# A hybrid decoder layer: attention as the second side stream, its gate first, gate transfers on GpSimd's queue, other pauses

## The chip, the cores and the metric

One core of a Trainium2 chip runs the whole kernel. The metric is the device time of one execution in microseconds, as the median of several runs. The engines are TensorE (PE), VectorE (DVE), ScalarE (ACT), GpSimd (POOL) and SyncE (SP, which here only issues DMAs).

## The reference

One decoder layer for 2048 prompt tokens and 8 x 4 sample tokens that share weights, all in float32:

```
proj = x @ w_in
q, k, v, g_a, u_b, g_b, x_c, g_c, g_m = split(proj)
attn = banded attention with sinks and relative bias, window 128     (branch a)
z    = gelu(S5 state space of u_b);  y_b = z * sigmoid(z @ w_glu)      (branch b)
y_c  = RG-LRU(causal conv4 of x_c)                                     (branch c)
ya = (attn * silu(g_a)) @ w_br_a;  yb = (y_b * silu(g_b)) @ w_br_b;  yc = (y_c * silu(g_c)) @ w_br_c
merged = sigmoid(g_m)[a] * ya + sigmoid(g_m)[b] * yb + sigmoid(g_m)[c] * yc
y = layernorm(alpha * x + merged @ w_out)
```

Outputs are y and the new caches and states.

## The kernel before

Float32 products are made of three passes: each operand is split into a high and a low part (`split`, L91 to L96: ACT makes the high part, DVE the low one), and `mm3` (L98 to L101) adds high by high, low by high and high by low.

Phase 1 is the input projection. `TILES` lists 50 tiles of 128 output columns; for each, `gemm` runs five units of tokens (512, 512, 512, 272, 272), each of 8 x 3 matmuls, with the tile's split weights against the split x, which stays in SBUF. `w_load` and `w_split` bring the next tile's weights (one "wh" on ACT and one "wl" on DVE a tile). `evac` empties PSUM: "m" tiles (the merge gates) take one ACT tanh and go to DRAM from ACT's queue; the gate tiles "gc", "gb", "ga" take an ACT tanh and two DVE products (one with PSUM, one with the branch's output, which `gate_load` has fetched into "br" a unit ahead), and go to DRAM with the next unit (`gate_st`). Both transfers are issued on SP (`LD`).

Beside it run four side streams, written as generators: `s5_stream`, `glu_stream`, `lru_stream`, `attn_stream`. Their matmuls are put between the main ones: after every three main matmuls `tick` adds their ideal time to a counter, and when it passes the pause that the last `yield` asked for (`STEP` 4.6 us where none is given), `side_step` runs the first stream in `sides` to its next `yield`. So the list `sides` and the pauses set the order of all queues; every engine then works in that order and waits by semaphores.

```
            sides += [glu_stream(), lru_stream(), attn_stream()]
```

An attention step `n` (block `n // 2`, key head `n % 2`) issues the scores of `n` ("sa", L1025 and L1026), the value products of `n - 2` ("sb", L1100, which read the copies "pth", "ptl", "ptq" that POOL masks), the transposes of `n - 1` ("sc", L1052, which read the softmax tile "S"), then DVE's maximum and sums, and yields `ATT_SCORE`; then ACT's exponentials and DVE's last product (`soft_norm`, L1012), and yields `ATT_SOFTMAX`. In odd steps `prep` also makes the high and low parts of the next block's queries and keys (the low parts "q" and "kl" on DVE). GLU runs 8 columns `j` in two halves; the first half of `j + 1` needs the split z ("zh", "zl") that `gelu_b` makes right behind the second half of `j`. RG-LRU makes 5 chunks of matmuls for each of 4 blocks, and then a chain of long ACT and DVE instructions with a scan of 2104 elements.

While the last gate runs, `seam` loads and splits the first branch's operands for phase 2 (`y_unit`: branch projections and merge) and phase 3 (`out_mm`, `out_ln`: output projection and layer norm).

Of the kernel before, what the change touches and what calls it, by code (L numbers as in the profile page):

```python
# [30 lines left out]
GLU_WEIGHTS = 2.0  # L31
ATT_SCORE, ATT_SOFTMAX = 2.5, 3.5
# [5 lines left out]
         + [("gc", i) for i in range(4)] + [("gb", i) for i in range(4)] + [("ga", i) for i in range(4)])  # L38
# [15 lines left out]
def kernel(ctx: ExitStack, tc: tile.TileContext, I, O):  # L54
# [62 lines left out]
    stage = ph1.enter_context(tc.tile_pool(name="stage", bufs=3))  # L117
# [20 lines left out]
    sides, a_done, prompt_done, pace, hold = [], [False], [False], [0.0, STEP], [0]  # L138
# [53 lines left out]
    def evac(kind, i, u, ps):  # L192
# [19 lines left out]
        elif kind == "q":  # L212
            spill(ps, n, qD[i][:, t0:t0 + n])
        elif kind == "m":
            spill(ps, n, mD[i][:, t0:t0 + n], AF.Tanh, 0.5)
        else:
            b = kind[1]
            gt = gp[0].tile([128, 512], FT, name=uid("gt"), tag="gt", bufs=2)[:, :n]
            br = gate_br.pop((b, i, u))
            act(gt, ps[:, :n], AF.Tanh, scale=0.5)  # L220
            stt(gt, gt, 1.0, ps[:, :n], OP.add, OP.mult)
            st = stage.tile([128, 512], FT, name=uid("st"), tag="st")[:, :n]
            if b == "b":
                nch = min(n, TP - t0) // 8
                V.tensor_mul(st[:, :nch * 8].rearrange("p (c j) -> p c j", j=8),
                             gt[:, :nch * 8].rearrange("p (c j) -> p c j", j=8),
                             br[:, :, 0:nch].rearrange("p j c -> p c j"))
                if u == 4:
                    V.tensor_mul(st[:, 240:272].rearrange("p (b t) -> p b t", t=4),
                                 gt[:, 240:272].rearrange("p (b t) -> p b t", t=4),  # L230
                                 br[:, 0:4, 30:38].rearrange("p t b -> p b t"))
            else:
                V.tensor_mul(st, gt, br)
            gate_st.append((actD[b][i][:, t0:t0 + n], st))
# [442 lines left out]
    def glu_stream():  # L677
# [58 lines left out]
        for j in range(8):  # L736
# [3 lines left out]
            yield  # L740
# [6 lines left out]
            yield  # L747
# [9 lines left out]
    def lru_stream():  # L757
# [123 lines left out]
        for i in range(4):  # L881
# [29 lines left out]
            stt(b_, b_, 0.5, R, OP.mult, OP.mult)  # L911
            V.memset(aa[:, 2048:2104].rearrange("p (b s) -> p b s", s=7)[:, :, 2], 0.0)
# [14 lines left out]
    def attn_stream():  # L927
        gp.append(side_pool(ges, "gate"))
# [219 lines left out]
        prompt_done[0] = True  # L1148
# [98 lines left out]
    def x_load(u):  # L1247
        t0, n = UN[u]
        for k in range(8):
# [3 lines left out]
            xr = early.tile([128, 512], FT, name=uid("xr"), tag="xr", bufs=6)  # L1253
# [7 lines left out]
    for kk in (slice(0, 4), slice(4, 8)):  # L1261
        r = early.tile([128, 512], FT, name=uid("xr"), tag="xr", bufs=6).rearrange("p (k c) -> p k c", k=4)
        LD.dma_start(r, I["w_in"][1][:, kk])
        split(WS[1][0][:, kk], WS[1][1][:, kk], r)
# [18 lines left out]
    BR = "cba"  # L1283
# [86 lines left out]

    def gate_load(b, i, u):
        t0, n = UN[u]
        br = gp[0].tile([128, 512], FT, name=uid("br"), tag="br", bufs=3)
        if b == "b":
            c0, nch = t0 // 8, 38 if u == 4 else n // 8
            br = br[:, :8 * nch].rearrange("p (j c) -> p j c", j=8)
            LD.dma_start(br, zD[i][:, :, c0:c0 + nch])
        else:
            br = br[:, :n]
            LD.dma_start(br, (hD if b == "c" else aD)[i][:, t0:t0 + n])  # L1380
# [3 lines left out]
    for i in range(2, len(TILES)):  # L1384
        kind, ti = TILES[i]
        if kind == "x" and ti == 0:
# [4 lines left out]
            sides += [glu_stream(), lru_stream(), attn_stream()]  # L1391
        if kind == "gc":
            while not gp:
                side_step()
        if kind == "ga":
            while not prompt_done[0]:
                side_step()
# [3 lines left out]
        for p, u in enumerate(order):  # L1401
            while gate_st:
                LD.dma_start(*gate_st.pop(0))
            if (kind, ti, p) == ("ga", 0, 3):
                while sides:
                    side_step()
# [9 lines left out]
            if kind == "ga":  # L1416
# [3 lines left out]
    while gate_st:  # L1420
        LD.dma_start(*gate_st.pop(0))
# [276 lines left out]
```

## Time and profile before

| | us |
|---|---|
| median of 3 runs | 1793.37 |
| lowest and highest | 1792.03, 1796.07 |
| the profiled execution | 1796.0 |
| its span, first to last instruction | 1793.9 |
| PE, DVE, ACT, POOL busy | 1771.1, 1132.4, 654.6, 169.5 |

The profiled execution is one run with the profiler on; the span is the part of it from its first to its last instruction, 2.1 us less. In the profile a busy PE includes the time in which a matmul waits behind its weight load, so its share says where the kernel is bound, and not that every matmul is at its peak. In this run side streams occupy these stretches: S5 to about 450 us, GLU 477 to 605, RG-LRU 622 to 838, attention 851 to 1160 and its sample part to 1240; the gates begin at about 1010 us.

### The profile page before, as it was taken

How to read it: one execution, taken by the hardware profiler on the slowest of the kernel's cores; microseconds unless marked ns; L12 is line 12 of the kernel's file. 1: busy time of each engine (PE TensorE's matmuls, PEld its weight loads, DVE VectorE, ACT ScalarE, POOL GpSimd, SP SyncE). 2: the span in 40 equal slices, each digit the busy share in tenths (PEclk: the TensorE clock that was granted, in tenths of full speed). 3: DMA queues.
4: the chain of work that ended last, by engine and by line, in shares of the span. 5: the costliest groups of instructions: out<-in, count | busy, mean ns of one | idle time of the engine just before them, and what ended most of it. 6: DMA issues, size and time to landing. Idle time of an engine off the chain costs nothing. (4 is left out here: it accounts for less than half of the span.)

```text
span 1793.9 us, 26547 instructions
## 1 busy us (share of the span) xinstructions
PE 1771.1 (99%) x9748; PEld 1543.1 (86%) x9748; DVE 1132.4 (63%) x2451; ACT 654.6 (36%) x1383; POOL 169.5 (9%) x379
## 2 busy tenths in 40 slices
PE   8999999999999999999999999999999999999997
PEld 7888888888899888888988888888888888887886
DVE  5755888886333456653777899653343557667666
ACT  6312443343333287674665655311220202111110
POOL 0000000000000000000355555400000000000000
PEclk9999999999999999999999999999999999999999
DMA  7443343433333334433332334453455646542222
GB/s 235 112 135 100 111 109 111 117 107 94 120 120 115 100 94 122 105 95 102 106 102 84 119 122 132 107 165 101 143 172 153 191 127 189 183 145 97 94 95 81
DMA packets 214278, 220.36 MB, mean 123 GB/s; under 512 B 89140, under 2 KB 157108, under 8 KB 212980
## 3 DMA queue, kind: packets, MB, share of 16 engines
q1 hardware_dynamic: 182772, 169.70, 33.4%
q10 hardware_dynamic: 31376, 48.97, 7.7%
q8 instruction: 77, 1.26, 0.3%
q14 instruction: 53, 0.43, 0.1%
HBM read 136.53 MB, written 83.14 MB: 122 GB/s over the span
## 5 line engine op out<-in xcount | busy, mean ns | idle before, releaser
L99 PE MATMUL mm<-xh,wh 128*128 128x512 f32 (+1 forms) x1920 | 678.8, 354 | 0.0
L101 PE MATMUL mm<-xh,wl 128*128 128x512 f32 (+1 forms) x1920 | 673.3, 351 | 0.0
L100 PE MATMUL mm<-xl,wh 128*128 128x512 f32 (+1 forms) x1920 | 671.1, 350 | 0.0
L101 PEld LDWEIGHTS mm<-xh,wl 128*128 128x128 f32 x1920 | 361.1, 188 | 47.1 <-DVE wl L94 0.3
L99 PEld LDWEIGHTS mm<-xh,wh 128*128 128x128 f32 x1920 | 361.6, 188 | 43.6
L100 PEld LDWEIGHTS mm<-xl,wh 128*128 128x128 f32 x1920 | 361.9, 188 | 42.7
L99 PE MATMUL py<-ah,wbh 128*128 128x512 f32 (+1 forms) x480 | 169.1, 352 | 1.5 <-DVE br L104 0.8
L101 PE MATMUL py<-ah,wbl 128*128 128x512 f32 (+1 forms) x480 | 168.9, 352 | 0.0
L100 PE MATMUL py<-ah,wbh 128*128 128x512 f32 (+1 forms) x480 | 168.8, 352 | 0.0
L89 ACT ACTIVATE st<-mm 128x512 f32<-128x512 f32 (+1 forms) x170 | 86.9, 511 | 155.9 <-PE mm L101 142.6
L99 PEld LDWEIGHTS py<-ah,wbh 128*128 128x128 f32 x480 | 90.3, 188 | 15.1 <-issue 1.1
L100 PEld LDWEIGHTS py<-ah,wbh 128*128 128x128 f32 x480 | 90.3, 188 | 12.7
L101 PEld LDWEIGHTS py<-ah,wbl 128*128 128x128 f32 x480 | 90.2, 188 | 12.5
L94 DVE TENSOR_TENSOR wl<-wr,wh 128x1024 fp32r<-128x1024 f32 x48 | 58.9, 1226 | 38.0 <-ACT wh L89 37.9
L1505 PE MATMUL po<-woh,mg 128*128 128x512 f32 x256 | 79.6, 389 | 0.0
L104 DVE SCALAR_TENSOR_TENSOR br<-br,py 128x512 f32<-128x512 f32 (+1 forms) x80 | 46.8, 585 | 51.5 <-PE py L101 45.7
L104 DVE SCALAR_TENSOR_TENSOR gt<-gt,mm 128x512 f32<-128x512 f32 (+1 forms) x60 | 35.0, 584 | 69.7 <-ACT gt L89 69.5
L89 ACT ACTIVATE gt<-mm 128x512 f32<-128x512 f32 (+1 forms) x60 | 30.9, 515 | 117.4 <-PE mm L101 117.4
L1505 PE MATMUL po<-woh,mo 128*128 128x512 f32 x224 | 69.5, 389 | 0.0
L89 ACT ACTIVATE wbh<-wbr 128x512 fp32r<-128x512 f32 x24 | 15.1, 629 | 147.7 <-PE py L100 125.7
L1543 POOL TENSOR_TENSOR lr<-lr,lngb 128x192 f32<-128x192 f32 x1 | 0.6, 589 | 628.8 <-ACT lr L1542 628.8
L89 ACT ACTIVATE wh<-wr 128x1024 fp32r<-128x1024 f32 x48 | 50.5, 1052 | 23.7 <-DMA wr<-in_w_in_dram 10.0
(352 smaller groups left out, 2797.2 us busy)
## 6 DMA issues: line engine op xcount, KB each, us to landing
wr<-in_w_in_dram SPq DMA_DIRECT2D x48, 512.0 KB
mD<-st ACTq DMA_DIRECT2D x72, 256.0 KB
br<-mD SPq DMA_DIRECT2D x71, 256.0 KB
lx<-in_xr_dram SPq DMA_DIRECT2D x16, 512.0 KB
mD<-st ACTq DMA_DIRECT2D x48, 136.0 KB
br<-mD SPq DMA_DIRECT2D x47, 136.0 KB
xr<-in_xT_dram SPq DMA_DIRECT2D x24, 256.0 KB
wbr<-in_w_br_dram SPq DMA_DIRECT2D x24, 256.0 KB
```

The lines of the kernel that those rows point to most:

```text
L89: return A.activation(out, in_, func, bias=bias, scale=scale, **kw)
L94: V.tensor_sub(lo, src, hi)
L99: PE.matmul(ps, wh, xh, start=start, stop=False)
L100: PE.matmul(ps, wh, xl, start=False, stop=False)
L101: PE.matmul(ps, wl, xh, start=False, stop=stop)
L104: return (eng or V).scalar_tensor_tensor(out, a, s, b, op0=op0, op1=op1)
L1505: PE.matmul(o, m, w, start=k == 0 and q == 0, stop=k == 7 and q + 1 == len(prods))
L1543: G.tensor_mul(r[:, c], r[:, c], gb[:, 0, c])
```

## The change

`sides` becomes attention, RG-LRU, GLU, and the gate tiles come as "ga", "gc", "gb", each after its stream. The first two gates have no pool of their own: their "br" and "gt" tiles come from the stage pool (now 4 tiles), the product is written in place, and both their transfers are issued on GpSimd's queue (`G`). Pauses change: GLU 4.6 to 3.9, attention 2.5 and 3.5 to 2.2 and 3.0. RG-LRU's end gets one more `yield`. The x start-up buffers go from 6 to 5. Phase 2 takes the branches as a, c, b.

```
-GLU_WEIGHTS = 2.0
-ATT_SCORE, ATT_SOFTMAX = 2.5, 3.5
+GLU_WEIGHTS, GLU_STEP = 2.0, 3.9
+ATT_SCORE, ATT_SOFTMAX = 2.2, 3.0
...
-         + [("gc", i) for i in range(4)] + [("gb", i) for i in range(4)] + [("ga", i) for i in range(4)])
+         + [("ga", i) for i in range(4)] + [("gc", i) for i in range(4)] + [("gb", i) for i in range(4)])
...
-    stage = ph1.enter_context(tc.tile_pool(name="stage", bufs=3))
+    stage = ph1.enter_context(tc.tile_pool(name="stage", bufs=4))
...
-            gt = gp[0].tile([128, 512], FT, name=uid("gt"), tag="gt", bufs=2)[:, :n]
+            early_ = not gp
+            gt = gate_tile("gt")[:, :n]
...
-            st = stage.tile([128, 512], FT, name=uid("st"), tag="st")[:, :n]
+            st = gt if early_ else stage.tile([128, 512], FT, name=uid("st"), tag="st")[:, :n]
...
-            gate_st.append((actD[b][i][:, t0:t0 + n], st))
+            gate_st.append((G if early_ else LD, actD[b][i][:, t0:t0 + n], st))
...
             glu_mm(j, 0)
...
-            yield
+            yield GLU_STEP
             glu_mm(j, 1)
...
-            yield
+            yield GLU_STEP
...
             stt(b_, b_, 0.5, R, OP.mult, OP.mult)
+            yield 2.5
...
-            xr = early.tile([128, 512], FT, name=uid("xr"), tag="xr", bufs=6)
+            xr = early.tile([128, 512], FT, name=uid("xr"), tag="xr", bufs=5)
...
-    BR = "cba"
+    BR = "acb"
...
+    def gate_tile(tag):
+
+        if not gp:
+            return stage.tile([128, 512], FT, name=uid("st"), tag="st")
+        return gp[0].tile([128, 512], FT, name=uid(tag), tag=tag, bufs=3 if tag == "br" else 2)
+
     def gate_load(b, i, u):
         t0, n = UN[u]
-        br = gp[0].tile([128, 512], FT, name=uid("br"), tag="br", bufs=3)
+        br = gate_tile("br")
+        q = LD if gp else G
...
-            LD.dma_start(br, (hD if b == "c" else aD)[i][:, t0:t0 + n])
+            q.dma_start(br, (hD if b == "c" else aD)[i][:, t0:t0 + n])
...
-            sides += [glu_stream(), lru_stream(), attn_stream()]
-        if kind == "gc":
-            while not gp:
+            sides += [attn_stream(), lru_stream(), glu_stream()]
+        if kind[0] == "g" and ti == 0:
+
+            while len(sides) > {"a": 2, "c": 1, "b": 0}[kind[1]]:
                 side_step()
-        if kind == "ga":
-            while not prompt_done[0]:
-                side_step()
+            if kind == "gb":
+                gp.append(side_pool(ges, "gate"))
```

How the built order moves, at three places. First DVE's queue in an odd attention step (the last half of step 21): "ptl" is the low part of the transposed softmax, "q" and "kl" the low parts of the next block, "m" the sums, "S" the softmax tile, "gt" and "st" a gate's two products, "wl" a weight split. Before:

```order
L1106 TENSOR_TENSOR oo_10977<-sb_11108,oo_10977 64x2x4x64
L1059 TENSOR_TENSOR ptl_11122<-sc_11116,pth_11121 128x512
L104 SCALAR_TENSOR_TENSOR q_11098<-qr_10914,q_11098 64x256 x2
L978 TENSOR_TENSOR kl_8514<-kr_10916,k_11100 64x256
L104 SCALAR_TENSOR_TENSOR q_11099<-qr_10914,q_11099 64x256 x2
L978 TENSOR_TENSOR kl_8515<-kr_10916,k_11101 64x256
L1010 TENSOR_TENSOR m_11097<-m_11097 128x4
L1011 RECIPROCAL m_11097<-m_11097 128x4
L1012 TENSOR_TENSOR S_11096<-S_11096,m_11097 128x4x128
L104 SCALAR_TENSOR_TENSOR gt_11192<-gt_11192,mm_11151 128x512
L233 TENSOR_TENSOR st_11195<-gt_11192,br_11032 128x512
```

With the change:

```order
L1107 TENSOR_TENSOR oo_7559<-sb_7670,oo_7559 64x2x4x64
L1060 TENSOR_TENSOR ptl_7684<-sc_7678,pth_7683 128x512
L104 SCALAR_TENSOR_TENSOR q_7660<-qr_7511,q_7660 64x256 x2
L979 TENSOR_TENSOR kl_5231<-kr_7513,k_7662 64x256
L104 SCALAR_TENSOR_TENSOR q_7661<-qr_7511,q_7661 64x256 x2
L979 TENSOR_TENSOR kl_5232<-kr_7513,k_7663 64x256
L94 TENSOR_TENSOR wl_7714<-wr_7380,wh_7713 128x1024
L1011 TENSOR_TENSOR m_7659<-m_7659 128x4
L1012 RECIPROCAL m_7659<-m_7659 128x4
L1013 TENSOR_TENSOR S_7658<-S_7658,m_7659 128x4x128
L1041 TENSOR_TENSOR S_7773<-sa_7764,B 128x768
```

The gate's two products between this step's softmax and the next step's first sum are gone, and in this step a weight split stands ahead of the sums; such a row stands there in two of the sixteen odd steps.

Second, DVE's queue around the place in GLU where the split z ("zl") of the next column is made; "zy" and "zt" are GLU's own tiles, "st" here a gate's. Before:

```order
L696 TENSOR_TENSOR zt_5756<-zt_5756,zy_5692 128x1056
L104 SCALAR_TENSOR_TENSOR zy_5561<-zs_5833,zy_5561 128x528
L104 SCALAR_TENSOR_TENSOR zy_5692<-zt_5756,zy_5692 128x1056
L96 SCALAR_TENSOR_TENSOR zl_5838<-zy_5692,zh_5837 128x1056
L94 TENSOR_TENSOR wl_5863<-wr_5643,wh_5862 128x1024
L104 SCALAR_TENSOR_TENSOR zy_5692<-zs_5901,zy_5692 128x528
L107 TENSOR_SCALAR zt_5904<-zt_5904 128x1056
L696 TENSOR_TENSOR zt_5904<-zt_5904,zy_5842 128x1056
```

With the change:

```order
L697 TENSOR_TENSOR zt_12034<-zt_12034,zy_11975 128x1056
L104 SCALAR_TENSOR_TENSOR zy_11716<-zs_12089,zy_11716 128x528
L104 SCALAR_TENSOR_TENSOR zy_11975<-zt_12034,zy_11975 128x1056
L96 SCALAR_TENSOR_TENSOR zl_12094<-zy_11975,zh_12093 128x1056
L104 SCALAR_TENSOR_TENSOR st_12105<-st_12105,mm_12042 128x512
L234 TENSOR_TENSOR st_12105<-st_12105,st_11935 128x512
L104 SCALAR_TENSOR_TENSOR zy_11975<-zs_12156,zy_11975 128x528
```

GLU's chain keeps its order, and a gate's two products follow it. PE has 24 main matmuls of 512 columns between two such GLU steps before and 21 now, where all of them are of that size; in an attention step between its scores and its transposes 30 before and 27 now.

Third, the issues of gate transfers. Before, on SP's queue beside attention ("oo" is attention's output):

```order
L1380 DMA br_10921<-hD 128x272
L1403 DMA actDc<-st_10951 128x272
L1380 DMA br_10954<-hD 128x512
L1403 DMA actDc<-st_11029 128x272
L1380 DMA br_11032<-hD 128x512
L1108 DMA aD<-oo_10977 128x4x128
L1403 DMA actDc<-st_11085 128x512
L1380 DMA br_11149<-hD 128x512
```

With the change, on POOL's queue, beside GLU:

```order
L1391 DMA st_12040<-hD 128x512
L1373 DMA actDc<-st_12105 128x512
L1391 DMA st_12110<-hD 128x272
L1373 DMA actDc<-st_12170 128x512
L1391 DMA st_12175<-hD 128x272
L1373 DMA actDc<-st_12202 128x272
```

Loads and stores of a gate alternate there with nothing else between; 80 of them leave SP.

## Rows read from the trace of the kernel before

**Rows 1.** The page, part 1: busy us, share of the span, instructions.
```profile
PE 1771.1 (99%) x9748; PEld 1543.1 (86%) x9748; DVE 1132.4 (63%) x2451; ACT 654.6 (36%) x1383; POOL 169.5 (9%) x379
```

**Rows 2.** Windows: from:to, length, then each engine's busy us, PEclk, DMA share, GB/s.
```profile
620.00:850.00 230.00, 230.00 (x1216) 199.46 (x1215) 125.95 (x161) 151.76 (x218) 0.91 (x5) 1.00 0.42 104
850.00:1000.00 150.00, 148.29 (x906) 132.37 (x904) 114.85 (x262) 91.17 (x277) 71.53 (x141) 1.00 0.32 99
1000.00:1150.00 150.00, 144.34 (x870) 127.83 (x869) 132.43 (x277) 82.48 (x262) 83.09 (x159) 1.00 0.40 120
1149.00:1152.00 3.00, 3.00 (x12) 2.71 (x12) 1.30 (x2) 1.19 (x2) 0.41 (x1) 0.51 0.45 87
...
1242.00:1246.00 4.00, 4.00 (x15) 3.19 (x14) 2.28 (x3) 0.60 (x1) 0.00 (x0) 0.73 0.00 0
```

**Rows 3.** Waits of PE: line, releaser, us in total, times, longest us.
```profile
PE sc L1052 <- DVE S L1012: 2.8, 5, 1.2
PE sb L1100 <- POOL ptl L1082: 1.7, 3, 1.2
PE sa L1025 <- ACT k L89: 1.0, 1, 1.0
...
PE sa L1026 <- DVE kl L978: 0.4, 1, 0.4
```

**Rows 4.** Timeline, an odd attention step beside "m": start us, us, engine, line, tiles.
```profile
932.82 0.27 PE L1026 MATMUL sa<-kl,q 128*128 128x192 f32 x1
...
936.42 0.39 PE L100 MATMUL mm<-xl,wh 128*128 128x512 f32 x1
...
936.64 0.39 PE L101 MATMUL mm<-xh,wl 128*128 128x512 f32 x1
...
940.25 0.95 POOL L1082 TENSOR_SCALAR_AFFINE_SELECT ptl<-ptl 64x256 fp32r<-64x256 f32 x2
...
941.10 0.69 DVE L1012 TENSOR_TENSOR S<-S,m 128x512 f32<-128x512 f32 x1
...
941.82 0.28 PE L1100 MATMUL sb<-ptl,vn 128*128 128x256 f32 x1
...
942.41 0.60 PE L1052 MATMUL sc<-ident,S 128*128 128x128 f32 x4
```

**Rows 5.** Timeline, an odd attention step beside a gate.
```profile
1042.99 1.22 DVE L94 TENSOR_TENSOR wl<-wr,wh 128x1024 fp32r<-128x1024 f32 x1 [0.72 <-ACT wh L89]
...
1044.13 0.68 DVE L104 SCALAR_TENSOR_TENSOR gt<-gt,mm 128x512 f32<-128x512 f32 x1
...
1044.85 1.03 DVE L233 TENSOR_TENSOR st<-gt,br 128x512 f32<-128x512 f32 x1
...
1053.58 0.69 DVE L1012 TENSOR_TENSOR S<-S,m 128x512 f32<-128x512 f32 x1
...
1053.84 0.30 PE L1100 MATMUL sb<-ptl,vn 128*128 128x256 f32 x1
...
1053.97 0.28 PE L1100 MATMUL sb<-ptq,vn 128*128 128x256 f32 x1
...
1054.42 0.63 PE L1052 MATMUL sc<-ident,S 128*128 128x128 f32 x4 [0.17 <-DVE S L1012]
```

**Rows 6.** Timeline, the gap between two GLU steps.
```profile
488.31 0.28 PE L101 MATMUL sb<-zh,glul 128*128 128x264 f32 x1
...
492.31 1.26 DVE L96 SCALAR_TENSOR_TENSOR zl<-zy,zh 128x1056 fp32r<-128x1056 f32 x1 [1.15 <-ACT zh L89]
...
493.90 0.28 PE L99 MATMUL sa<-zh,gluh 128*128 128x264 f32 x1
```

**Rows 7.** Timeline, the start.
```profile
1.26 0.89 SPq L1254 DMA_DIRECT2D xr<-in_xT_dram  x2
...
4.21 1.29 ACT L89 ACTIVATE xh<-xr 128x512 fp32r<-128x512 f32 x2 [0.61 <-DMA xr<-in_xT_dram]
...
12.52 1.34 DVE L94 TENSOR_TENSOR w<-xr,w 128x512 fp32r<-128x512 f32 x2
```

More of the change, by code (lines that the diff above doesn't have):

```diff
@@ L134 @@
         X[u] = (xhp.tile([128, 8, n], FR, name=f"xh{u}", tag=f"xh{u}"), xlp.tile([128, 8, n], FR, name=f"xl{u}"))
-    sides, a_done, prompt_done, pace, hold = [], [False], [False], [0.0, STEP], [0]
+    sides, a_done, pace, hold = [], [False], [0.0, STEP], [0]
     def side_step():
@@ L927, in attn_stream @@
     def attn_stream():
-        gp.append(side_pool(ges, "gate"))
         es = ExitStack()
@@ L1147, in attn_stream @@
         es.close()
-        prompt_done[0] = True
         es = ExitStack()
@@ L1261 @@
     for kk in (slice(0, 4), slice(4, 8)):
-        r = early.tile([128, 512], FT, name=uid("xr"), tag="xr", bufs=6).rearrange("p (k c) -> p k c", k=4)
+        r = early.tile([128, 512], FT, name=uid("xr"), tag="xr", bufs=5).rearrange("p (k c) -> p k c", k=4)
         LD.dma_start(r, I["w_in"][1][:, kk])
@@ L1369, with gate_store @@
     gate_br, gate_st = {}, []
+    def gate_store():
+        q, dst, src = gate_st.pop(0)
+        q.dma_start(dst, src)
+    def gate_tile(tag):
+        if not gp:
+            return stage.tile([128, 512], FT, name=uid("st"), tag="st")
+        return gp[0].tile([128, 512], FT, name=uid(tag), tag=tag, bufs=3 if tag == "br" else 2)
     def gate_load(b, i, u):
         t0, n = UN[u]
-        br = gp[0].tile([128, 512], FT, name=uid("br"), tag="br", bufs=3)
+        br = gate_tile("br")
+        q = LD if gp else G
         if b == "b":
@@ L1376, in gate_load @@
             br = br[:, :8 * nch].rearrange("p (j c) -> p j c", j=8)
-            LD.dma_start(br, zD[i][:, :, c0:c0 + nch])
+            q.dma_start(br, zD[i][:, :, c0:c0 + nch])
         else:
             br = br[:, :n]
-            LD.dma_start(br, (hD if b == "c" else aD)[i][:, t0:t0 + n])
+            q.dma_start(br, (hD if b == "c" else aD)[i][:, t0:t0 + n])
         gate_br[(b, i, u)] = br
@@ L1402 @@
             while gate_st:
[L1403 to L1406, printed above, removed]
+                gate_store()
             if kind[0] == "g" and (p < 4 or ti < 3):
@@ L1415 @@
             evac(kind, ti, u, ps)
-            if kind == "ga":
+            if kind == "gb":
                 seam(ti, u)
@@ L1420 @@
     while gate_st:
-        LD.dma_start(*gate_st.pop(0))
+        gate_store()
     ph1.close()
```

## The prediction

> **What bounds the kernel now.** I read the page's shares first, then the windows by stage, then TensorE's waits, and last the timeline around one step of each side stream. The shares say that TensorE (PE) is busy for 1771.1 us of a span of 1793.9 us [rows 1]; all matmuls of the kernel remain, so a reordering can only touch the 22.8 us that are left and what is hidden inside the busy time. The windows say where it is [rows 2]: RG-LRU (620 to 850 us) leaves PE no idle time at all; attention leaves 1.71 us in 150 while it runs beside the "m" tiles and 5.66 us in 150 while it runs beside the gates. The waits name the releasers [rows 3]: the softmax tile S from VectorE (DVE) and the masked copies ptl from GpSimd (POOL), eight times together, and 1.4 us once at attention's first score matmul. So the kernel is PE-bound to 99%, and the question is how many short waits of an in-order PE queue the new order removes and how many it makes.
>
> One attention step shows the mechanism. In an odd step beside "m" [rows 4] the last score matmul ends at 933.09, DVE then works through maximum, sums, the low parts of the next block and the last softmax product, which ends at 941.79: 8.70 us of DVE. The transposes that need it start at 942.41, so 0.62 us are spare. Beside a gate [rows 5] the DVE queue first holds a weight split (1.22), the gate's two products (0.68 and 1.03), and the same chain ends at 1054.27, 11.3 us after that split began; PE stood and started 0.15 us later.
>
> **The change, part by part.** PE's matmuls keep their number. Main matmuls of 512 columns start 0.22 us apart [rows 4]; I take 0.227.
>
> *Attention moves beside "m" and ahead of all gates.* Its waits before: idle 1.71 + 5.66 - 1.4 (the first score, which comes again) = 6.0 us [rows 2, 3]. A wait as shown is shorter than what it costs: 0.17 is shown at 1054.42, while two rows that normally start 0.12 apart started 0.45 apart, which makes 0.33 [rows 5]. Between that 0.15 and about 0.3 a piece, over some ten waits, I take 2.8. After the longest wait the granted clock was 0.51 for 3 us (1149 to 1152), which is 1.5 us [rows 2]. Together 10.3 us that the old place costs.
>
> *The pauses of attention fall from 2.5 and 3.5 to 2.2 and 3.0.* Pauses are spent in groups of three matmuls, so in the order this is 30 main matmuls of 512 columns between a step's scores and its transposes before, and 27 now: 0.68 us less room. With the spare 0.62, less 0.15 for the hand-over, an odd step is late by 0.2 us; even steps have no low parts and keep spare room. Fifteen odd steps give 3.0 us. In two of them the new order puts a weight split between the low parts and the last product (shown above), and 1.22 us comes on top each time: 2.5. Together 5.5. From below, 2.5, if the row I chose is tighter than most; from above, 0.6 a step, if POOL's copies are late as well: their last rows end at 941.20, so the product that reads them at 941.82 had 0.6 to spare, and that room shrinks by the same 0.68 [rows 4]. That is 9 + 2.5 = 11.5. Attention nets 5.5 - 10.3 = -4.8, between -7.8 and +1.2.
>
> *GLU's pause falls from 4.6 to 3.9, and GLU runs beside the "gc" gate.* From the last GLU matmul (ends 488.59) to the end of zl (493.57) is a chain of 4.98 us on ACT and DVE, and the next GLU matmuls start at 493.90, 5.31 us after [rows 6]. So there is a third of a microsecond to spare, with 24 main matmuls of 512 columns between. The new order has 21 there, in five of the seven places where zl is new: the gap is 4.63. The second matmul, 0.12 later, needs zl, which with the hand-over comes at 5.13: 0.38 us of waiting, five times. In the two other places 272-column matmuls fill the gap, worth 4.3 us: about 0.7 each. Sum 1.9 + 1.4 = 3.3 us where there was nothing. The gate's DVE products stand behind zl in the queue (shown above), so they add nothing to the chain as long as their operand has landed.
>
> *RG-LRU's last row of blocks runs beside "ga".* PE waited for nothing there [rows 2], but four gaps now share DVE with two gate products. They fit into DVE's waits for ACT; I take 0.5 us, between 0 and 4 x 1.7 = 6.8 if each fell into the chain. The extra pause after the two long products costs PE nothing and lets a gate's products in before the scan.
>
> *Gate transfers from GpSimd's queue.* Eighty DMA issues leave SP and stand on POOL, whose attention work is over by then, so nothing but other gate transfers queues behind them. Behind a late load stands a gate product on DVE, and behind that GLU's and RG-LRU's work. The trace has no DMA issued from POOL. The nearest rows: two issues on SP took 0.89 us, and the data of the first were in use 2.95 us after it began [rows 7]. A gate load is issued once the product two units earlier has freed its tile, some 5 us ahead of its use even in the short 272-column units. Taken: 0, because 2.95 is far below 5. A gain of the sort that SP gets free is 0 too: no PE wait is on an SP load in that stretch [rows 3]. The upper end is a rival below. The Trainium skill speaks against this part: "SBUF — State Buffer", the section SBUF: two separate sides, has it that GpSimd can't write a DMA's descriptors while DVE runs a two-port operation, and gives some 620 ns against 3100 ns for one DMA. By that rule, as an estimate, about 2.5 us would come on top, and a load would just reach its use; no trace here has such a DMA yet.
>
> *Five start-up buffers instead of six.* The sixth load waits for the first buffer. The split of the second weight tile ends at 13.86 when the first round of matmuls is over [rows 7]; it comes up to 1 us later. I take 0.4, between 0 and 1. The gate order a, c, b, the fourth stage tile and the "gb" seam leave PE's work as it is, hidden by matmuls as the "ga" seam was: 0.
>
> **Sum.** -4.8 + 3.3 + 0.5 + 0.4 = -0.6 us, against the profiled execution's 1796.0: 1795.4. That execution lies 2.6 us above the median of the runs, so on the median of 1793.37 it is **1792.8**. A measurement of this kernel tells about 0.2%, 3.6 us, from no change; the forecast is that there is none to tell.
>
> **Rivals.**
> *Attention's waits go almost all, and GLU alone pays.* Two weight splits (2.5) remain, and the stretch at a lower clock after the small sample matmuls (0.73 granted over the 4 us from 1242, which is 1.1 us) goes too [rows 2]. -10.3 + 2.5 - 1.1 + 3.3 + 0.9 = -4.7: 1788.7. For it: spare room varies from step to step. Against it: DVE has 8.7 us of work where about 8.7 of room is left.
> *The shorter pauses make attention late in every odd step (slower).* The place is the transposes behind DVE's last softmax product; the price is 11.5 us against 10.3 before; it decides from a DVE chain of more than about 9 us, or POOL copies later by 0.3. +1.2 + 3.3 + 0.9 = +5.4: 1798.8. For it: DVE was busy 115 of 150 us beside "m" at the longer pauses [rows 2]. Against it: no gate products are in the queue now.
> *GpSimd's loads land late.* If a load takes over 5 us from issue to landing, each microsecond beyond it passes through DVE into seven GLU places and four RG-LRU gaps: 11 us at 1 us late, so 1803.8. For it: no row shows how fast POOL issues a load beside a DVE that GLU keeps busy. Against it: 2.95 us on SP. The Trainium skill's rule, cited with the gate transfers, would lead here.
> That a gate waits for an unfinished stream by force would show as steps packed together; in the order every stream ends before its gate, so I give it nothing.
>
> **How the numbers follow.** Forecast 0.47, its own range 1789.8 to 1797.0; attention free 0.28; attention late 0.14; late loads 0.11. So faster 0.28, within 0.2% 0.47, slower 0.25. The range goes from a little below the first rival, 1787, to a little above the second, 1799.5; the late loads lie outside, and half a tenth below.
>
> **What would show it.** In the changed profile: PE's idle time beside attention near 5 us with S L1013 as the releaser in odd steps; a new PE wait on zl in front of GLU matmuls, some seven times 0.3 to 0.7; no DVE wait on the DMAs of "ga" and "gc". PE busy time should stay at 1771 us. The forecast is wrong if the waits on S exceed 10 us, if zl is not waited for, or if DVE waits for a gate load.

## The result, and the profile after the change

The changed kernel takes 1811.93 us (median of 5 runs, 1809.89 to 1813.93) against 1795.3 us for the kernel before in the same comparison. The ratio is 1.0089, with a 95% interval from 1.0078 to 1.0101: slower by 0.9%, 16.6 us. The forecast was 1792.8, in a range up to 1799.5. The profiled execution took 1812.72 us, with a span of 1811.0, 17.1 more than before.

The page, part 1, of the kernel after (busy us, share of the span, instructions):

```profile
PE 1777.9 (98%) x9748; PEld 1546.6 (85%) x9748; DVE 1133.5 (63%) x2451; ACT 654.9 (36%) x1383; POOL 209.7 (12%) x459
```

The same number of matmuls is busy 6.8 us longer than in [rows 1], and the span holds 10.3 us more in which PE is idle. The 80 new instructions on POOL are the gates' DMA issues. PE's waits of the kernel after (line, releaser, us in total, times, longest), the list that answers to [rows 3]:

```profile
PE mm L99 <- DVE st L104: 6.3, 1, 6.3
...
PE sc L1053 <- DVE S L1013: 2.6, 10, 0.5
PE sa L100 <- DVE zl L96: 2.2, 5, 0.8
PE sa L888 <- ACT ig L89: 2.0, 2, 1.4
PE sb L1101 <- POOL ptl L1083: 0.9, 3, 0.4
```

Left out are the wait of the first matmuls for x, which the kernel before has too, and two waits of under 0.5 us. The waits on S and zl that the prediction named are there. The first line is new: a main matmul that waits 6.3 us, once, for a gate's evacuation. The windows by stage (from:to, length, then PE, PEld, DVE, ACT, POOL busy, PEclk, DMA share, GB/s) say where:

```profile
450.00:600.00 150.00, 148.61 (x891) 131.59 (x890) 109.04 (x249) 86.90 (x268) 67.24 (x133) 1.00 0.32 98
600.00:750.00 150.00, 147.49 (x900) 130.86 (x899) 115.67 (x252) 87.41 (x273) 88.32 (x179) 1.00 0.29 91
...
850.00:1050.00 200.00, 197.90 (x1049) 170.89 (x1048) 119.19 (x163) 138.29 (x205) 8.02 (x17) 1.00 0.42 111
1050.00:1110.00 60.00, 53.68 (x286) 46.88 (x285) 31.55 (x38) 19.79 (x25) 12.88 (x24) 0.94 0.51 154
...
1084.00:1092.00 8.00, 4.14 (x11) 3.32 (x12) 4.58 (x8) 3.06 (x6) 2.14 (x4) 0.57 0.72 248
```

The first two rows are attention, now beside "m" alone: 3.9 us idle where [rows 2] had 7.4 in its two 150 us windows. The fourth row is the hand-over from RG-LRU to GLU beside "ga": 6.3 us idle in 60 us, and a granted clock of 0.57 in the 8 us around it (last row). The timeline shows the hand-over, and behind the last line of dots the end of the program:

```profile
1067.88 4.54 DVE L916 TENSOR_TENSOR_SCAN R<-a,xf 128x2104 f32<-128x2104 f32 x1
...
1072.49 0.33 SPq L919 DMA_DIRECT2D hD<-R  x1
...
1073.71 0.68 DVE L104 SCALAR_TENSOR_TENSOR st<-st,mm 128x512 f32<-128x512 f32 x1
...
1079.21 0.81 SPq L725 DMA_DIRECT2D zy<-in_w_glu_dram  x2
...
1085.85 0.63 ACT L89 ACTIVATE gluh<-zy 128x512 fp32r<-128x512 f32 x1 [10.05 <-DMA zy<-in_w_glu_dram]
1086.39 0.58 ACT L89 ACTIVATE st<-mm 128x512 f32<-128x512 f32 x1
...
1087.12 0.68 DVE L104 SCALAR_TENSOR_TENSOR st<-st,mm 128x512 f32<-128x512 f32 x1
...
1087.86 0.80 PE L99 MATMUL mm<-xh,wh 128*128 128x512 f32 x1 [6.32 <-DVE st L104]
...
1803.33 0.34 ACTq L1543 DMA_DIRECT2D out_y_dram<-lr  x1
```

Read it from the bottom up. PE at 1087.86 needs a PSUM buffer that the gate's product at 1087.12 frees; that needs the gate's tanh at 1086.39; the tanh stands in ACT's queue behind "gluh", the split of GLU's weights, which waited 10.05 us for its load; and the load was issued only at 1079.21, because its memory was RG-LRU's until the stores of 1072.49 and after had read it. SP's own waits name the last of them:

```profile
SPq L725 <- DMA out_lru_p_dram<-R: 3.7, 1, 3.7
```

Behind the gap PE's matmuls take 0.80 and 0.63 and not 0.39 us: the granted clock is at its lower level (1.2 of 2.4 GHz) for some 7 us, the last 3 of the wait and the first 4 of the work after it.

The last row says something else. After ACT's last DMA issue at 1803.33 the span runs 7.7 us on. In the kernel before, the same instruction has this row, and the span of 1793.9 ends 3.9 us after it:

```profile
1789.99 0.34 ACTq L1535 DMA_DIRECT2D out_y_dram<-lr  x1
```

To add everything up I took, for each pair of neighbouring matmuls, the distance between their starts less the usual distance of two matmuls of these sizes (the tenth percentile in the kernel before; 0.226 us for two of 512 columns), and summed this by stretch, each from a stream's first matmul to the next one's. It holds waits, lower clock and small delays alike. Each column is one profile; the sample part, which most of the edits below leave as it is, differs by some 3 us among their profiles, as the lower clock is granted there for a longer or shorter time:

| stretch | before, us | after, us | change | in the prediction |
|---|---|---|---|---|
| start-up and S5 | 10.9 | 11.4 | +0.4 | +0.4 |
| attention | 26.0 | 22.4 | -3.6 | -4.8 |
| sample part and what follows it | 5.8 | 6.5 | +0.7 | 0 |
| RG-LRU, up to GLU's first matmul | 3.4 | 15.4 | +12.0 | +0.5 |
| GLU, up to the next stream or phase 2 | 2.5 | 7.8 | +5.2 | +3.3 |
| phases 2 and 3 | 10.2 | 8.9 | -1.3 | 0 |
| end, after the last matmul | 9.0 | 12.7 | +3.7 | 0 |

The changes add up to the 17.1 us of the spans. Two places carry what was not foreseen: RG-LRU's stretch and the program's end.

### The profile page after: what moved, and what is told of

Same layout as the page of the kernel before. It is cut to its first block, busy times and chain, and to the rows that moved or that the text cites. A ratio compares the mean times of both kernels' runs of the same rounds, so it can differ in the third digit from the quotient of the medians.

```text
span 1811.0 us, 26639 instructions
## 1 busy us (share of the span) xinstructions
PE 1777.9 (98%) x9748; PEld 1546.6 (85%) x9748; DVE 1133.5 (63%) x2451; ACT 654.9 (36%) x1383; POOL 209.7 (12%) x459
## 3 DMA queue, kind: packets, MB, share of 16 engines
q0 software_dynamic: 5376, 17.04, 3.1%
## 5 line engine op out<-in xcount | busy, mean ns | idle before, releaser
L89 ACT ACTIVATE st<-mm 128x512 f32<-128x512 f32 (+1 forms) x210 | 107.3, 511 | 267.0 <-PE mm L101 234.6
L100 PEld LDWEIGHTS py<-ah,wbh 128*128 128x128 f32 x480 | 90.4, 188 | 12.7
L89 ACT ACTIVATE wh<-wr 128x1024 fp32r<-128x1024 f32 x48 | 50.6, 1054 | 25.4 <-DMA wr<-in_w_in_dram 10.1
L1513 PEld LDWEIGHTS po<-woh,mg 128*128 128x128 f32 x256 | 48.1, 188 | 9.9
L104 DVE SCALAR_TENSOR_TENSOR acc<-br,py 128x512 f32<-128x512 f32 (+1 forms) x38 | 22.3, 589 | 51.1 <-PE py L101 48.9
```

What stands on the lines that cost most here:

```text
L89: return A.activation(out, in_, func, bias=bias, scale=scale, **kw)
L100: PE.matmul(ps, wh, xl, start=False, stop=False)
L104: return (eng or V).scalar_tensor_tensor(out, a, s, b, op0=op0, op1=op1)
L1513: PE.matmul(o, m, w, start=k == 0 and q == 0, stop=k == 7 and q + 1 == len(prods))
```

## The experiments

All are edits of the changed kernel, but for one_pool_dma, which edits the kernel before. The comparisons are with the kernel before on the same chip; the stretches are sums as above, and the end is here the time from the last DMA issue on ACT's queue to the end of the span.

| kernel | us | ratio to before | attention | RG-LRU | GLU | end |
|---|---|---|---|---|---|---|
| before | 1793.4 | | 26.0 | 3.4 | 2.5 | 3.9 |
| after | 1811.9 | 1.0089 [1.0078, 1.0101] | 22.4 | 15.4 | 7.8 | 7.7 |
| e1_gates_sp | 1819.2 | 1.0131 [1.0111, 1.0152] | 22.4 | 25.2 | 7.2 | 3.9 |
| e2_glu46 | 1806.0 | 1.0067 [1.0053, 1.0080] | 22.3 | 16.5 | 3.6 | 7.7 |
| e3_late_glu | 1804.7 | 1.0054 [1.0041, 1.0067] | 22.3 | 6.7 | 10.0 | 7.7 |
| e4_one_pool_dma | 1793.0 | 0.9993 [0.9983, 1.0003] | 24.1 | 3.5 | 2.5 | 3.8 |
| e5_both | 1801.3 | 1.0042 [1.0029, 1.0054] | 22.4 | 6.7 | 5.7 | 7.7 |
| e6_both_stores_sp | 1807.9 | 1.0078 [1.0065, 1.0091] | 22.4 | 18.9 | 3.3 | 4.3 |
| e7_att_pauses | 1804.7 | 1.0057 [1.0044, 1.0070] | 15.0 | 15.9 | 7.6 | 7.7 |
| e8_no_lru_pause | 1813.9 | 1.0106 [1.0091, 1.0121] | 22.4 | 10.1 | 14.6 | 7.8 |
| e9_gc_sp | 1807.4 | 1.0066 [1.0054, 1.0079] | 22.3 | 14.2 | 7.2 | 4.3 |
| e10_best | 1803.5 | 1.0043 [1.0028, 1.0057] | 16.7 | 14.8 | 8.6 | 4.3 |
| e11_best_gcpool | 1807.4 | 1.0066 [1.0054, 1.0079] | 16.6 | 15.6 | 11.3 | 7.7 |
| e12_ga_earlier | 1820.7 | 1.0144 [1.0131, 1.0157] | 22.3 | 22.2 | 7.7 | 7.4 |
| e13_ga_earlier_rest | 1802.3 | 1.0037 [1.0024, 1.0051] | 16.6 | 14.8 | 7.1 | 4.3 |
| e14_no_ga_products | 1810.4 | 1.0082 [1.0069, 1.0095] | 22.6 | 14.3 | 8.2 | 7.7 |
| e15_phase | 1787.5 | 0.9966 [0.9955, 0.9977] | 16.6 | 4.0 | 4.9 | 4.3 |
| e16_pool60 | 1810.2 (one run) | | 22.4 | 14.8 | 8.0 | 5.7 |
| e17_pool120 | 1805.8 (one run) | | 22.4 | 14.5 | 7.8 | 4.3 |

### The hand-over: a later weight split

```
             SD.dma_start(gr[i], I["w_glu"][:, 2 * i:2 * i + 2])
         yield
+        yield
+        yield
```

> The changed kernel with two more pauses of 4.6 us between the issue of GLU's weight load and the first split of these weights. Theory A (the split gluh stands ahead of the gate's tanh in ScalarE's queue, and its load is late): PE's wait of 6.3 us on st and the stretch at half clock after it (some 3 us) go, time about 1803. Rival D (RG-LRU's last products on VectorE alone hold the gate up, and the load only shares the place): PE still stands 4 us or more within 10 us of that place, time 1809 or more.

Measured: PE's wait on "st" and the stretch at the lower clock are gone, RG-LRU's stretch falls from 15.4 to 6.7, and the time to 1804.7. GLU's stretch grew by 2.2, with eight waits on "zl" in place of five; that its steps now fall otherwise against the gate's units is the likely reason, and no run isolates it. Theory A holds; rival D would have left 4 us of waiting.

### The hand-over: the gate's products taken away

```
-            stt(gt, gt, 1.0, ps[:, :n], OP.add, OP.mult)
+            if b != "a":
+                stt(gt, gt, 1.0, ps[:, :n], OP.add, OP.mult)
...
-            else:
+            elif b != "a":
                 V.tensor_mul(st, gt, br)
```

> The changed kernel with gate ga's two products on VectorE left out: its tanh goes to memory as it is, and the loads of attention's output are not read. If the gate's products behind RG-LRU's tail on VectorE are what keeps the buffers full: PE's wait at the hand-over falls below 2 us, time about 1804. If it is the order of ScalarE's queue (late GLU weights ahead of the tanh): PE still waits 4 to 6 us there, now on ScalarE's st, time 1809 to 1812.

Measured: 1810.4. The timeline at the hand-over of this kernel:

```profile
1083.59 0.63 ACT L89 ACTIVATE gluh<-zy 128x512 fp32r<-128x512 f32 x1 [16.02 <-DMA zy<-in_w_glu_dram]
1084.12 0.58 ACT L89 ACTIVATE st<-mm 128x512 f32<-128x512 f32 x1
...
1084.76 0.79 PE L99 MATMUL mm<-xh,wh 128*128 128x512 f32 x1 [6.38 <-ACT st L89]
```

With no gate product on DVE, PE waits as long as with them, 6.4 us, now for ACT's tanh itself. What costs is the order of ACT's queue with a late load at its head: PE has three PSUM buffers, here for units of 512, 272 and 272 tokens, and all three stay full until "gluh" is done. RG-LRU's long DVE tail had delayed one gate product to 1073.71, but that is not what PE stood for.

### GLU's pause

```
-GLU_WEIGHTS, GLU_STEP = 2.0, 3.9
+GLU_WEIGHTS, GLU_STEP = 2.0, 4.6
```

> The changed kernel with GLU's pause at 4.6 us as before. If the pause alone makes PE wait for zl: the five waits (2.2 us shown, some 4 to 5 us of start-to-start gaps) go, time about 1807.5, GLU some 10 us longer in the program but still ended ahead of gb. Rival (gate products ahead of zl on VectorE make it late): the zl waits stay, under 1 us of change.

Measured: 1806.0, and no wait on "zl" is left. GLU's stretch falls from 7.8 to 3.6, so the shorter pause cost 4.1 us there.

### Both

The two edits above (e3's and e2's) at once.

> The changed kernel with both edits at once: GLU's pause at 4.6 us and two more pauses ahead of GLU's weight split. If they are separate losses, the gains add: 1811.9 less 5.9 less 7.2 is 1798.8, and lower by up to 1.5 where the waits on zl that the later split brought along go too. Rival: GLU now ends in the last main matmuls ahead of gb, whose first loads need its output; then PE waits at gb's start and 2 us or more are given back, 1801 or more.

Measured: 1801.3, some 2.5 above the sum of the single gains. The wait on "st" is gone, RG-LRU's stretch stays at 6.7, and GLU's stands at 5.7, above the 3.6 of the pause alone. The gains nearly add. The time lies in the rival's range (1801 or more), but the rival's place, PE at the start of "gb", has no wait.

### Attention's pauses

```
-ATT_SCORE, ATT_SOFTMAX = 2.2, 3.0
+ATT_SCORE, ATT_SOFTMAX = 2.5, 3.5
```

> The changed kernel with attention's pauses at 2.5 and 3.5 us as before; GLU then ends 24 main matmuls later, still ahead of gb. The prediction's term (odd steps late by what the pauses lost): the ten waits on S and three on ptl go, 3.5 us shown and 4 to 5 us in all, time about 1807.5. Rival E (these waits cost what they show, or come from weight splits, so one or two remain): a gain of under 2 us, 1810 to 1812. Rival F (the hand-over from RG-LRU to GLU, now in another tile, is worse there): 1813 or more.

Measured: 1804.7. Windows of this kernel over attention:

```profile
450.00:600.00 150.00, 150.00 (x911) 134.27 (x910) 104.26 (x236) 82.50 (x252) 62.30 (x125) 1.00 0.33 101
600.00:750.00 150.00, 149.64 (x926) 134.34 (x925) 115.09 (x252) 89.33 (x279) 82.26 (x168) 1.00 0.29 90
```

PE has 0.4 us idle where the changed kernel has 3.9, with 46 more matmuls in the same 300 us. The sum of the stretch falls from 22.4 to 15.0. The prediction's account of odd steps holds, and its price was too low: the thirteen waits on S and "ptl" show 3.5 us, the distances right at them hold 5.7 more than usual, and the stretch 7.4. This also splits attention's term: the move beside "m" gave 26.0 - 15.0 = 11.0 us, and the shorter pauses took 7.4 of it back. The 11.0 is good to some 2 us: e4_one_pool_dma, whose attention is that of the kernel before, has 24.1 and no stretch at the lower clock. Rival E falls; rival F does too (6.2 us on "st" again).

### Transfers on the two queues

e1_gates_sp issues all of "ga" and "gc" on SP, e6_both_stores_sp (on top of e5_both) only their stores, e9_gc_sp only "gc":

```
-        q = LD if gp else G
+        q = LD
...
-            gate_st.append((G if early_ else LD, actD[b][i][:, t0:t0 + n], st))
+            gate_st.append((LD, actD[b][i][:, t0:t0 + n], st))
```

> The changed kernel with the transfers of the gates ga and gc issued on SyncE's queue again; all else as changed. Theory A (the loss is the hand-over from RG-LRU to GLU beside ga, and the end after the last output DMA grows by 3.7 us because DMAs of GpSimd's queue exist): the 6.3 us wait of PE on st L104 stays, the end shrinks from 12.7 to 9.0 us after the last matmul, time about 1808. Theory B (late loads and stores of GpSimd's queue are the whole cost): about 1795, no wait on st. Theory C (SyncE's queue is worse here, since gate loads then stand behind the loads of RG-LRU's and GLU's streams, which wait for memory): new DVE waits on gate loads, 1815 or more.

Measured: 1819.2, slower than the changed kernel by 7. The timeline of this kernel beside "ga":

```profile
1020.31 1.07 SPq L1391 DMA_DIRECT2D st<-aD  x2
...
1027.27 0.69 DVE L234 TENSOR_TENSOR st<-st,st 128x512 f32<-128x512 f32 x1 [8.11 <-DMA st<-aD]
...
1027.99 1.40 DVE L865 TENSOR_TENSOR f<-xf,f 64x512 fp32r<-64x512 f32 x2
...
1028.82 1.42 PE L888 MATMUL sa<-f,lwh 128*128 128x512 f32 x2 [4.14 <-DVE f L865]
```

The gate loads of 1020.31 stand on SP's queue behind RG-LRU's four stores, which begin at 1017.22, when the scan of its third row is done. So a gate product waits 8.11 us for its load, RG-LRU's "f" stands behind it on DVE, and PE behind "f". RG-LRU's stretch grew by 9.8, against 3.7 gained at the end. Theory C holds for "ga", though with stores ahead of the loads, and A for the end and for the hand-over (5.6 us on "st"); as the only loss of the change (B), GpSimd's queue is ruled out.

> As the kernel with both edits, and the gates' stores on SyncE's queue, so that 40 transfers and not 80 are left on GpSimd's. If the longer end grows with the number of such transfers: 12.7 us after the last matmul become 10.8, and the time falls by 1.9. If it is there whole as soon as there are more than a few: 12.7 stay. Theory C' (a store that waits for VectorE on SyncE's queue holds up RG-LRU's loads behind it): waits of PE on f L865 return and the time grows by 2 us or more.

Measured: 1807.9, 6.6 slower than e5_both. The end falls by 3.4, more than expected, and PE waits 7.6 us on "ig" in RG-LRU: C' in kind, on ACT's "ig" and not on "f". ACT's tanh at 1037.43 waits 8.22 us for a gate store, and RG-LRU's "f" and "ig" stand behind it on ACT.

> The changed kernel with the transfers of gate gc alone on SyncE's queue, so that 40 are left on GpSimd's, 20 loads and 20 stores of ga. If the longer end is set by the number of transfers on GpSimd's queue, it comes out as in the kernel with 40 loads there (9.3 us after the last matmul): time 1808.5. Rival (it is the stores on that queue that lengthen the end): 10.8 us or more. If SyncE's queue holds up GLU as it held up RG-LRU: new waits of PE on zl or zh beside gc, and no gain.

Measured: 1807.4; the end falls to 4.3, with 20 stores still on GpSimd's queue, so stores are not its cause. GLU's stretch is 7.2 against 7.8: beside these pauses SP's queue carries "gc" as well as GpSimd's does.

### The program's end

In the kernel before, one store goes to GpSimd's queue:

```
-        SD.dma_start(O["ssm_p"], hf)
+        G.dma_start(O["ssm_p"], hf)
```

> The kernel before, with a single small store (the state output ssm_p) issued on GpSimd's queue and not on SyncE's. If the longer end is a fixed cost of a program that has any DMA on that queue: the end after the last output DMA grows by about 3.7 us and the time by the same, 1799. Rival (the end grows with the number of such DMAs, 80 in the changed kernel): under 0.3 us, 1795.3. Third way (the longer end has another cause, such as other clocks or memory places): no change either, and the end of the gates-on-SyncE kernel stays long.

Measured: 1793.0, ratio 0.9993 [0.9983, 1.0003]; the end stays (3.8). One transfer costs nothing. With 60 and 120:

```
-        q = LD if gp else G
+        q = G if b == "a" or b == "c" and i < 2 else LD
```

> The changed kernel with gate ga and the first two tiles of gc on GpSimd's queue, 60 transfers. A slope from 40 to 80 gives 11.0 us after the last matmul; a step gives 9.3 or 12.7.

The second has `q = G` throughout, and stores likewise.

> The changed kernel with all three gates on GpSimd's queue, 120 transfers. If the end grows with the number beyond 40: 16.2 us after the last matmul; if it is a step: 12.7.

Measured: after the last matmul 10.8 us with 60, as on a slope between 40 and 80, but 9.3 with 120, where the slope would give 16.2. From ACT's last DMA issue to the end that is 3.9 us with none and 3.8 with one, 4.3 with 40 (five kernels), 5.7 with 60, 7.4 to 7.8 with 80 (nine kernels), and 4.3 with 120; 60 and 120 were run once each. The traces name the wait. On the program's last line each engine has a DRAIN, and the others stand until GpSimd's is over. GpSimd's row in the kernel before, in the changed kernel (80 transfers) and with 120 (ns min/median/max, first and last start; the longest of the three is the one that counts):

```profile
L1684 POOLq DRAIN  x3: 34/78/951, 1789.1 to 1793.7; - x3
```

```profile
L1692 POOLq DRAIN  x3: 40/102/7509, 1802.4 to 1810.7; - x3
```

```profile
L1692 POOLq DRAIN  x3: 45/102/2612, 1798.9 to 1803.8; - x3
```

It lasts 0.95 us with none, 4.24 with 40, 5.88 with 60 and 7.51 with 80: 82 ns more for each transfer, and the same within 3 ns in all kernels with the same number. It begins 0.9 us ahead of ACT's last issue, and SP is done 3.5 us behind that issue; so with 40 transfers the DRAIN is hidden, and with 80 the program waits some 3 us for it. With 120 it lasts 2.61 us, as some 20 transfers would; why so little stays open.

### RG-LRU's extra pause

```
-            yield 2.5
             V.memset(aa[:, 2048:2104].rearrange("p (b s) -> p b s", s=7)[:, :, 2], 0.0)
```

> The changed kernel without the extra pause of 2.5 us in RG-LRU's end. The prediction's value (it costs and gives nothing): within 1.5 us of 1811.9. Rival (the pause is what lets a gate's products in ahead of the scan on VectorE): without it PE's wait on st L104 grows from 6.3 us to 8 or more, 1814 or more. Third way (GLU and its load come earlier, away from the gate's tanh): the wait on st falls below 4 us, 1808 or less.

Measured: 1813.9, 2 us above the changed kernel, with intervals that overlap, so neither clearly nothing nor a loss. The wait of 6.3 us is gone, as in the third way: GLU's load comes earlier, and "gluh" waits 2.4 us for it. The 2.8 us on "st" that PE has left are another wait, at 1060.18, behind the scan of RG-LRU's fourth row (from 1054.78, 4.54 us), which is the rival's place. GLU's stretch grew to 14.6: its first matmul now waits 2.5 us for "zh", and eight others wait for "zl" (3.4 us).

### Where "ga" stands against RG-LRU

The first attempt to gather all mends (the pause in odd steps, GLU's two pauses apart, the later split, "gc" on SP) and the same with "gc" left on GpSimd's queue:

```
-            yield ATT_SOFTMAX
+            yield 3.5 if n % 2 else ATT_SOFTMAX
...
                 gelu_a(j + 1)
-            yield GLU_STEP
+            yield 3.2
...
                 load(j + 2)
-            yield GLU_STEP
+            yield 4.6
...
-        q = LD if gp else G
+        q = G if b == "a" else LD
```

> The changed kernel with all that the runs point to: attention's second pause 3.5 us in odd steps and 3.0 in even ones, GLU's pauses 3.2 ahead of a column's second half and 4.6 ahead of its first, two more pauses ahead of GLU's weight split, gate gc on SyncE's queue. From 1801.3 of the kernel with both edits: attention's waits 5 to 7 less, the end 3.4 less, GLU's rest 1 to 2 less: 1790, faster than before by 3 to 4. If the prediction's account of odd steps is wrong (even steps wait as much at 3.0): the ten waits on S fall to five, 1793. If the gains overlap: 1795.

> As the last kernel, with gate gc left on GpSimd's queue: the same up to the end, which is 3.4 us longer. If GpSimd's queue also helps or hurts GLU, the stretch beside gc differs by more than 1 us.

Measured: 1803.5 and 1807.4, far above the forecast. Attention's stretch did what was expected (16.7; three waits on S of 0.9 us in all, so most of the late steps were odd ones), and the second kernel is 3.9 slower, 3.4 of it at the end. Its GLU stretch is 2.7 longer, above the 1 us that the expectation set, so "gc" on GpSimd's queue may cost something here; its profiled execution is its longest, 2.5 above its median. But RG-LRU's stretch rose to 14.8. The timeline of e10_best beside "ga":

```profile
1015.52 4.54 DVE L918 TENSOR_TENSOR_SCAN R<-a,xf 128x2104 f32<-128x2104 f32 x1
...
1021.91 0.55 POOL L1375 DMA_DIRECT2D actDa<-st  x1 [11.51 <-DVE st L234]
...
1022.46 0.54 POOL L1393 DMA_DIRECT2D st<-aD  x1
...
1029.58 0.44 DVE L234 TENSOR_TENSOR st<-st,st 128x272 f32<-128x272 f32 x1 [4.88 <-DMA st<-aD]
...
1030.88 1.42 PE L890 MATMUL sa<-f,lwh 128*128 128x512 f32 x2 [3.00 <-DVE f L867]
...
1080.62 0.50 PE L99 MATMUL mm<-xh,wh 128*128 128x512 f32 x1 [2.84 <-DVE st L104]
```

The scan of the third row holds up a gate product, and with it the store on GpSimd's queue, which waits 11.51 us for DVE. Right behind that store stands the next gate load, of 1022.46. It lands 7.0 us after its issue; the gate's product waits 4.88 us for it, RG-LRU's "f" for DVE, and PE for "f". The last row is PE behind the scan of the fourth row. RG-LRU began 72 main matmuls later than in the changed kernel, and the scan of its third row begins 21 us after the first gate load, there 10.5 us. So the place counts. Two kernels put "ga" four tiles earlier:

```
-         + [("m", i) for i in range(24)]
-         + [("ga", i) for i in range(4)] + [("gc", i) for i in range(4)] + [("gb", i) for i in range(4)])
+         + [("m", i) for i in range(20)] + [("ga", i) for i in range(4)] + [("m", i) for i in range(20, 24)]
+         + [("gc", i) for i in range(4)] + [("gb", i) for i in range(4)])
```

> The changed kernel with the last four m tiles between ga and gc, so that ga runs beside the steady part of RG-LRU and the hand-over to GLU beside m tiles. Theory A (the hand-over beside a gate is the loss): PE's wait on st and the half clock after it go, some 8 us; ga beside RG-LRU's steps costs 0 to 3: time 1804 to 1807. Rival (RG-LRU's steps don't bear a gate either, each with two more VectorE products): waits of PE on ig and f over 6 us in all, 1810 or more.

> The last kernel with the other mends: attention's second pause 3.5 us in odd steps, GLU's pauses 3.2 and 4.6, gate gc on SyncE's queue. Under theory A: the last kernel less 5 for attention, 3.4 for the end and 3 to 4 for GLU, some 1793. Under the rival: 1799 or more.

Measured: 1820.7 and 1802.3. Theory A in this form falls, and both times are in the rival's range; of the rival's waits 4.1 us on "ig" are there and none on "f". The timeline of e12_ga_earlier:

```profile
957.58 4.54 DVE L916 TENSOR_TENSOR_SCAN R<-a,xf 128x2104 f32<-128x2104 f32 x1
962.25 0.68 DVE L104 SCALAR_TENSOR_TENSOR st<-st,mm 128x512 f32<-128x512 f32 x1
962.98 0.80 PE L99 MATMUL mm<-xh,wh 128*128 128x512 f32 x1 [2.84 <-DVE st L104]
...
976.82 1.22 PE L888 MATMUL sa<-f,lwh 128*128 128x512 f32 x2 [3.57 <-ACT ig L89]
...
1095.11 0.79 PE L99 MATMUL mm<-xh,wh 128*128 128x512 f32 x1 [4.93 <-ACT st L89]
```

Here "ga" meets a whole row of RG-LRU: behind the scan a gate product comes late and PE waits 2.84, then 3.57 on "ig". And the hand-over, now beside "m" tiles, still costs 4.93: ACT's queue with the late weights at its head is nearly as bad beside tiles without any DVE product.

So the last kernel takes e5_both, with "gc" on SP and 3.5 us in odd attention steps, and cuts five pauses between attention and RG-LRU's first step, so that RG-LRU starts about where it did:

```
-        yield
+        yield 2.5
```

> The changed kernel with the later GLU split, GLU's pause 4.6, gate gc on SyncE's queue, attention's second pause 3.5 us in odd steps, and five pauses between attention's last softmax and RG-LRU's first step cut from 4.6 to 2.5 us, so that RG-LRU's steps stand against the units of ga as in the kernel with both edits (its first matmul after 3781 main matmuls, there some 10 more). If the place against ga is what counts: 1801.3 less 5.7 for attention and 3.4 for the end, 1792 to 1793, with waits of PE on ig of 2 us and none on st. If the cut pauses make the sample part or RG-LRU's start late: new waits there, 1795 or more. If RG-LRU beside ga is late wherever it stands: waits on f, ig or st of 4 us or more beside ga, 1797 or more.

Measured: 1787.53 us (7 runs, 1786.72 to 1791.0), ratio 0.9966 [0.9955, 0.9977]: faster than the kernel before by 0.34%, than the changed one by 24 us, and some 5 below what was expected: the waits on "ig", which were to stay, are gone too. PE's waits of this kernel are complete in these lines:

```profile
PE mm L99 <- ACT xh L89: 5.4, 1, 5.4
PE sa L100 <- DVE zl L96: 1.1, 2, 0.7
PE sc L1055 <- DVE S L1015: 0.9, 3, 0.4
PE sb L1103 <- POOL ptl L1085: 0.2, 1, 0.2
```

Its windows over RG-LRU and the hand-over:

```profile
850.00:1050.00 200.00, 200.00 (x1082) 174.55 (x1081) 115.22 (x157) 139.24 (x202) 11.23 (x23) 1.00 0.44 115
1050.00:1110.00 60.00, 60.00 (x328) 52.58 (x327) 36.87 (x46) 18.04 (x27) 10.76 (x20) 1.00 0.56 168
```

Of the 8.4 us of idle time that the changed kernel has in these two windows nothing is left. The timeline of this kernel where "ga" begins:

```profile
999.02 4.54 DVE L918 TENSOR_TENSOR_SCAN R<-a,xf 128x2104 f32<-128x2104 f32 x1
...
1006.13 0.69 DVE L104 SCALAR_TENSOR_TENSOR st<-st,mm 128x512 f32<-128x512 f32 x1 [1.19 <-ACT st L89]
```

The third row's scan ends at 1003.6, ahead of the gate's first product. Ahead of GLU this kernel differs from e10_best only in the five cut pauses, and RG-LRU's stretch is 4.0 and not 14.8. DVE still waits for gate loads in both, three times each (9.2 us here, 7.6 in e10_best), so late loads alone don't make the loss. What RG-LRU pays beside "ga" hangs on where its row tails fall against the gate's units.

## Why the prediction was wrong, point by point

**What bounds the kernel** was read rightly: PE, with short waits in an in-order queue. That PE's busy time would stay at 1771 was wrong: it is 1777.9. Matmuls at the lower clock last longer, but by the distances of starts that is under 2 of the 6.8 us (5.4 against 3.7 in the kernel before); the rest is added at the full granted clock, in attention, RG-LRU and GLU.

**Attention, -4.8: measured -3.6, inside its bounds,** with two errors that partly cancel. The gain of the old place was put at 10.3 and is 11.0; the cost of the shorter pauses at 5.5 and is 7.4. Ten waits on S, 0.26 us each on average, are the odd steps' 0.2; that a wait costs more than its row shows was said, but taken as too little.

**GLU's pause, +3.3: the pause cost 4.1.** Mechanism, place and number are as forecast (waits on "zl", gone at 4.6): the list counts five, with up to 0.8, and in the two other places the same matmul starts 0.3 us late. The whole stretch is 5.2 longer; 1.1 of it stay with the pause of 4.6.

**RG-LRU's last row beside "ga", +0.5: measured +12.0. This is the step that failed.** It priced the gate's two DVE products in four gaps, with 6.8 us as the bound, and nothing else; the hand-over to GLU has no term in its sum. The larger part, 8.7 us by e3_late_glu, is a step that the change moves and that the prediction passed over: the load and split of GLU's weights now follow RG-LRU's end. The load waits for RG-LRU's memory, and the split stands ahead of a main tile's evacuation in ACT's queue. In the kernel before, the same split also waited for its load (its row, and what ended ACT's idle time before it):

```profile
L89 ACT ACTIVATE gluh<-zy x4: 616/632/634, 459.9 to 463.0; 128x512 fp32r<-128x512 f32 x4
...
  DMA zy<-in_w_glu_dram: 7.0, 1
```

PE had no wait there. The row should have been costed at the new place, where RG-LRU's stores hold the load up longer and ACT waits 10.05 us. The rest, 3.3 us, which e3_late_glu still has, is RG-LRU beside a gate, and e15_phase shows that its place decides.

**Gate transfers, 0: in RG-LRU and GLU right, at the end wrong by 3.7.** The rival of late GpSimd loads fell in the form it was given. The line of the gate loads in the kernel after (issues by form: ns min/median/max, first and last start; waits for them; time from issue to landing):

```profile
L1391 POOL DMA_DIRECT2D st<-aD x20: 536/536/722, 1001.0 to 1109.2; - x20
L1391 POOL DMA_DIRECT2D st<-hD x20: 536/536/538, 1117.9 to 1250.1; - x20
...
  DVE st L234: 1.6, 1
...
DMA to landing us min/median/max: 2.6/3.4/7.6
```

An issue takes 0.54 us, a load 3.4 us in the median, under the 5 us from which the rival decided; seven of the forty took longer. DVE waited for one once, 1.6 us: by the letter one of the prediction's signs of being wrong, but no wait of PE stands behind it. The Trainium skill's rule ("SBUF — State Buffer", SBUF: two separate sides), by which about 2.5 us were estimated on top of the 2.95 on SP, would make that 5.4 us, past the 5 and not just in time as the prediction says; the trace doesn't agree for the typical load, though the slowest took 7.6. The slow one of e10_best (7.0 us) was under way while DVE stood idle for 4.9 us; what made it slow is not shown. And SP's queue, the alternative, costs some 10 us beside RG-LRU (e1_gates_sp). For the end of the program the prediction has no term; there GpSimd's closing DRAIN lasts 7.51 us and not 0.95.

**Start-up, +0.4** agrees for start-up and S5 together, though the sixteen profiles of edits of the changed kernel have their first stretch, up to S5's first matmul, 0.3 to 1.9 us above the 4.9 of the kernel before (e4_one_pool_dma, with six buffers, 0.2), so the fewer buffers cost about 1 us rather than 0.4. **The "gb" seam and the branch order, 0**: phases 2 and 3 took 1.3 less; no run isolates it.

**The rivals.** "Attention late in every odd step" is near what happened in attention (7.4, between the forecast's 5.5 and its own 11.5), but gave only 2 us of the miss. None of the rivals was the hand-over or the end.

## What to carry to other kernels

When streams are reordered, price each seam between two neighbours anew: the first load of the next stream waits for the last stream's memory, and whatever waits for that load stands at the head of an in-order queue that also empties PSUM; put some steps between a load and its first use (8.7 us here). A wait that was harmless in the old place is a row to cost, not to skip. And a gain in one stream shifts all that follow, so after each mend check where the long tails of a later stream fall, as the five cut pauses show (14.8 against 4.0 us).

## What the runs showed of the hardware that was not expected

GpSimd's closing DRAIN grows with the number of DMA transfers that were issued on its queue hundreds of microseconds earlier: 0.95 us with none, 1.05 with one, 4.24 with 40, 5.88 with 60 and 7.51 with 80, so 82 ns for each. The time shows it only where it outlasts the other queues' last work: 4.3 us from ACT's last DMA issue to the end with 40 against 3.9 with none, but 7.4 to 7.8 with 80. With 120 it is 2.61 us again. The queue moved 25.63 MB there and 17.04 MB with 80, so the size of the data doesn't set it.

A wait of PE of 6.3 us went with some 7 us at the lower granted clock (0.57 over 1084 to 1092), so the hand-over cost 8.7 us where its row shows 6.3. The thirteen short waits of attention, 3.5 us in their rows, cost 5.7 us in the distances right at them without any fall of the clock (1.00 in both windows).
